# The end of the first norm moved from GpSimd to VectorE, in place, and the first expert's input taken straight from the selection product

## The chip, the cores and the metric

One core of one Trainium2 chip runs the kernel. TensorE multiplies matrices, VectorE and ScalarE work on elements, GpSimd does some element work and issues DMAs, and the sync engine's queue issues the large loads. The metric is device time in microseconds for one execution; lower is better.

## The reference, cut to what matters

One layer on 512 tokens of 1024 features (16 more tokens are prepended and cut off again). Two mixers give `mixed`, and then:

```python
h = layer_norm(ALPHA * h + mixed @ w_out, ln1_g, ln1_b)      # the first norm
logits_g, logits_e = h @ w_rg + b_rg, h @ w_re + b_re        # one of 4 groups, 2 of its 4 experts
...
for e in range(16):
    y = y + gates[:, e:e + 1] * ((silu(h @ w1[e]) * (h @ w3[e])) @ w2[e])
h = layer_norm(ALPHA * h + y, ln2_g, ln2_b)
```

The kernel computes an expert only for the tokens that chose it (up to 128 slots).

## The kernel before, in words

Everything is float32. To multiply at full rate each operand is split into two parts, high and low, and a product is three matmuls (`mm3`, lines 128 to 130). For the experts' weights a split is one ScalarE copy (line 900) and one VectorE subtraction (line 901) of 128 x 1024 elements. The kernel is written in program order under a tile framework, which inserts the waits between engines and whose scheduler orders the instructions of each engine by its own estimates; `issue_after` holds a block of instructions back until a given one.

The stages are: the input projection woven with the first mixer; the second mixer (`stick_breaking`, with scans at line 513 on VectorE) woven with the output projection (`out_proj`); the end of the first norm, the router and the choice of experts; 16 experts; the second norm.

Tokens come in four row blocks of 128. Blocks 3 and 2 end inside the weave, blocks 1 and 0 behind it. For each block `out_second` adds the last half of the projection to the rows `r` (line 743), transposes `r` on TensorE for the router's product (lines 750 to 754), takes mean and deviation (`norm_stats`, lines 249 to 253, with a logarithm and an exponential on ScalarE), corrects the router's logits (lines 757 and 758), and rewrites `r` as (r - mean) / deviation (line 759, VectorE). `out_rows` then makes gain and bias on GpSimd (lines 762 and 763, each 128 x 1024 elements) into another tile, `h1`, and writes it to two arrays in DRAM: `h1d`, from which the experts gather their tokens, and `ad`, to which they add their results. `choose` finds the experts of two blocks (lines 778 to 791, VectorE), `rank` numbers the tokens of an expert (two TensorE matmuls and lines 807 and 809); line 809 builds `sf`, the selection of expert 0's tokens.

Expert 0 does not gather. `first_rows` (line 923, TensorE) multiplies the rows by `sf`, which selects and transposes them at once; line 1197 (VectorE, eight instructions) gives gain and bias to the product, and lines 1199 and 1200 split it into `xh` and `xl`. Expert 1 gathers its tokens by the index of line 957 (line 963, GpSimd), and line 1031 transposes them on TensorE. Behind expert 0's first product all engines pass a branch (line 1088) that handles experts with more than 128 tokens; it reads a count that line 1002 writes, and ScalarE reaches it behind the activation at line 1050.

The weights come in loads of 1 MB on the sync engine's queue (`pump`, line 877) into 15 slots, at most three in flight. A slot is free again when its two parts are split (`split_to`), so the splits set when loads start.

Of the kernel before, what the change touches and what calls it, by code (L numbers as in the profile page):

```python
# [9 lines left out]
F32 = mybir.dt.float32  # L10
# [3 lines left out]
AF = mybir.ActivationFunctionType  # L14
OP = mybir.AluOpType
# [3 lines left out]
P = 128  # L19
D = 1024  # L20
# [3 lines left out]
KC = D // P  # L24
# [21 lines left out]
FIRST = 4  # L46
# [35 lines left out]
def hymba_kernel(ctx: ExitStack, tc: tile.TileContext, x, meta, w_in, lbnd, hgg, sbg, w_out, ln1g, ln1b,  # L82
                 wrg, brg, wre, bre, wg, wu, wd, ln2g, ln2b, out):
    nc = tc.nc
    V = nc.vector
# [4 lines left out]
    def f32(ap):  # L90
        return ap.bitcast(F32)
# [17 lines left out]
    h1d = tc.dram_tile([T, D], F32, name="h1d")  # L109

    ad = tc.dram_tile([T, D], F32, name="ad")
# [79 lines left out]
    for i2 in range(2):  # L191
        xr_ = xr[i2]
        for i1 in range(2):
            i = 2 * i2 + i1
            for hf in range(2):
                p_ = pj([P, 4, P])
# [512 lines left out]
    rt_ = []  # L709
# [29 lines left out]
    def out_second(i, acc, first):  # L739
        r = rt_[i]  # L740
        for hf in range(2):
            cs = slice(hf * 512, hf * 512 + 512)
            V.tensor_add(r[:, cs], r[:, cs], acc[hf])
        if i % 2 == first:
            h1[i], h1[i ^ 1] = (t[:, j] for t in (big_tile(2),) for j in range(2))
        hT = h1[i].rearrange("p (a b) -> p a b", a=KC)
        for hf in range(2):
            p_ = zb([P, 4, P])
            for k in range(4):
                nc.tensor.transpose(p_[:, k, :], r[:, (4 * hf + k) * P:(4 * hf + k + 1) * P], ident)  # L750
            nc.scalar.activation(hT[:, 4 * hf:4 * hf + 4], p_, AF.Copy)
        p_ = zb([P, 20])
        for k in range(KC):
            nc.tensor.matmul(p_, hT[:, k, :], wr[:, k, :], start=(k == 0), stop=(k == KC - 1))
        mu, rstd = norm_stats(r)

        V.scalar_tensor_tensor(lg[:, i, :], nws, mu, p_, op0=OP.mult, op1=OP.add)
        V.scalar_tensor_tensor(lg[:, i, :], lg[:, i, :], rstd, lgb, op0=OP.mult, op1=OP.add)
        V.tensor_scalar(r, r, mu, rstd, op0=OP.subtract, op1=OP.mult)

    def out_rows(i):
        nc.gpsimd.tensor_mul(h1[i], rt_[i], gb1[0])
        nc.gpsimd.tensor_add(h1[i], h1[i], gb1[1])
        nc.gpsimd.dma_start(h1d[i * P:(i + 1) * P, :], h1[i])
        nc.gpsimd.dma_start(ad[i * P:(i + 1) * P, :], h1[i])

    cnt, ohg, M = small("cnt", [NT, 5, 4]), small("ohg", [NT, 4]), small("M", [2, NT, 4, 4])
    Mb = small("Mb", [NT, NE], BF)
# [2 lines left out]
    def choose(i0):  # L771

        sl = slice(i0, i0 + 2)

        l5 = lg[:, sl].rearrange("p i (r j) -> p (i r) j", j=4)
        lj, li = l5[:, :, None, :].to_broadcast([P, 10, 4, 4]), l5[:, :, :, None].to_broadcast([P, 10, 4, 4])
        gt4, ge4 = (ctl.tile([P, 10, 4, 4], F32, tag="gt", bufs=2, name="gt") for _ in range(2))
        V.tensor_tensor(gt4, lj, li, op=OP.is_gt)
        V.tensor_tensor(ge4, lj, li, op=OP.is_ge)
        V.copy_predicated(gt4.rearrange("p a b c -> p a (b c)"),  # L780
                          before.rearrange("p a b -> p (a b)")[:, None, :].to_broadcast([P, 10, 16]),
                          ge4.rearrange("p a b c -> p a (b c)"))
        V.tensor_reduce(cnt[:, sl].rearrange("p i r j -> p (i r) j"), gt4, axis=AX.X, op=OP.add)
        V.tensor_scalar(ohg[:, sl], cnt[:, sl, 0, :], 0.0, None, op0=OP.is_equal)
        ohgb = ohg[:, sl, :, None].to_broadcast([P, 2, 4, 4])
        top = ctl.tile([P, 2, 4, 4], F32, tag="top", bufs=1, name="top")
        V.tensor_scalar(top, cnt[:, sl, 1:5, :], 1.0, None, op0=OP.is_le)
        V.tensor_mul(Mb[:, sl].rearrange("p i (g e) -> p i g e", g=4), top, ohgb)

        V.tensor_scalar(M[:, 1, sl], cnt[:, sl, 1:5, :], 1.0, None, op0=OP.is_equal)  # L790
        V.tensor_mul(M[:, 1, sl], M[:, 1, sl], ohgb)

    r1, sf = small("r1", [NT, NE]), [None, None]

# [20 lines left out]
    def out_proj():  # L815
        gb = big_tile(2)
        gb1.extend((bcast_row(gb[:, 0], ln1g, nc.scalar), bcast_row(gb[:, 1], ln1b, nc.scalar)))
        wo = wo_half(0)
        yield 1
        for i in range(NT):  # L820
            if i % 2 == 0:
                t = big_tile(2)
                rt_.extend((t[:, 0], t[:, 1]))
            nc.sync.dma_start(rt_[i], x[0, i * P:(i + 1) * P, :])
            acc = [zb(), zb()]
            for n_ in range(4):
                wo_mm(i, 0, wo, acc, (n_,))
                if n_ < 3:
                    yield 1
            for hf in range(2):  # L830
                cs = slice(hf * 512, hf * 512 + 512)
                V.scalar_tensor_tensor(rt_[i][:, cs], rt_[i][:, cs], ALPHA, acc[hf], op0=OP.mult, op1=OP.add)
            yield 1
        wo = wo_half(4)
        pump(R_LATE)
        yield 1
        wo2.extend(wo)
        for i in (3, 2):
            acc = [zb(), zb()]
            for n_ in range(4):  # L840
                wo_mm(i, 4, wo, acc, (n_,))
                yield 1
            out_second(i, acc, 1)
            out_rows(i)
            yield 1
        choose(2)
        rank(2)
        pump(R_AFTER)
# [63 lines left out]
    for i in (0, 1):  # L912
        wo_mm(i, 4, wo2, acc2[i], range(EARLY, 4))
    for i in (0, 1):
        out_second(i, acc2[i], 0)

    p1_ = [pj([P, 4, P]) for _ in range(2)]

# [6 lines left out]

    for hf in range(2):
        first_rows(hf, 1)
    choose(0)
    nc.gpsimd.memset(xg, 0.0)
    pump(R_NEXT - at[0])  # L930

# [7 lines left out]
    def select(e):  # L939

        s_ = mp.tile([P, NT, P], BF, tag="sel", bufs=3, name="sel")
        V.tensor_tensor(s_, iow[:, None, :].to_broadcast([P, NT, P]), r1[:, :, e:e + 1].to_broadcast([P, NT, P]),
                        op=OP.is_equal)
        return s_
# [140 lines left out]
    def overflow():  # L1085

        n_max = nc.values_load(cmi[0:1, 0:1], min_val=0, max_val=T)
        with tc.If(n_max > CAP):  # L1088
            with ExitStack() as ov:
# [44 lines left out]
                with tc.For_i(0, NE, 1) as e:  # L1134
                    for c in range(1, T // CAP):
# [40 lines left out]
                                                 scale=osv[:, 1:2].bitcast(F32))  # L1176
                        scatter(y, osv[:, 0:1])

    sel1 = select(1)
    with tc.issue_after(i_.ins):  # L1180
        split_to(FIRST)
    xh = mp.tile([P, KC, P], F32R, tag="xh", bufs=1, name="xh")
    xl = mp.tile([P, KC, P], F32R, tag="xl", bufs=1, name="xl")
    x1 = mp.tile([P, D], F32, tag="y", bufs=1, name="y").rearrange("p (k n) -> p k n", k=KC)
    for hf in range(2):
        first_rows(hf, 0)
        p_ = p1_[hf]
        if hf == 0:
            p1 = slot_sums(1, sel1, slice(0, 2))
            slot_rows(1, p1)  # L1190
            with tc.issue_after(i_.ins):
                out_rows(0)
                out_rows(1)
            gather(xg[:, 1], idx[:, 1:2])
        for k in range(4):
            c = 4 * hf + k
            V.tensor_scalar(x1[:, c], p_[:, k], cp[:, 16 + c:17 + c], cp[:, 24 + c:25 + c], op0=OP.mult, op1=OP.add)
        d_ = slice(4 * hf, 4 * hf + 4)
        nc.scalar.activation(xh[:, d_], x1[:, d_], AF.Copy)
        V.tensor_sub(xl[:, d_], x1[:, d_], f32(xh[:, d_]))  # L1200
    xs[0] = (xh, xl)
    gscr = mp.tile([P, 512], F32, tag="hs", bufs=1, name="gscr")
    gscr = (gscr[:, 0:2 * NT * NE], gscr[:, 2 * NT * NE:4 * NT * NE])
# [216 lines left out]
```

## Time and profile before

| | |
|---|---|
| median of 3 runs | 730.28 us (729.41 to 730.34) |
| the profiled execution | 727.62 us, its span 725.9 us |
| PE (TensorE) busy | 658.3 us, 91% of the span |
| DVE (VectorE) busy | 550.8 us, 76% |
| ACT (ScalarE) busy | 426.0 us, 59% |
| POOL (GpSimd) busy | 189.3 us, 26% |
| DMA | 143.67 MB, mean 198 GB/s |

The profile gives each engine's busy time, the granted TensorE clock, the transfers, and who waited for whom. Busy shares are averages over stages with different limits, so the text reads the stage around the change by itself. A busy VectorE instruction may also be one that is held up: its duration then stands out against the same instruction elsewhere.

### The profile page before, as it was taken

The page shows a single profiled execution, that of the slowest core. Times are in us where ns is not written, and L with a number is a line of the kernel's source. Part 1 is how long each engine was busy: PE and PEld are TensorE (multiplying, and loading weights), DVE is VectorE, ACT ScalarE, POOL GpSimd, SP SyncE. Part 2 cuts the span into 40 slices and gives each one's busy share as a digit, 9 for nine tenths or more (in the row PEclk, how much of TensorE's full clock was granted, in tenths as well). Part 3 has the DMA queues.
Part 4 walks back from the last instruction along what each step waited for, and adds up shares of the span by engine and source line. Part 5 has one row for each costly group of instructions (what it writes and reads, how often), then busy time and mean ns, then how long its engine had stood idle before and what let it go on. Part 6 is the DMA issues. An engine that isn't in the chain of part 4 may idle for free. (4 is left out here: it accounts for less than half of the span.)

```text
span 725.9 us, 9414 instructions
## 1 busy us (share of the span) xinstructions
PE 658.3 (91%) x3366; PEld 530.3 (73%) x3366; DVE 550.8 (76%) x851; ACT 426.0 (59%) x640; POOL 189.3 (26%) x187
## 2 busy tenths in 40 slices
PE   6999999999999999988775799999999999999870
PEld 5878878777877777777665688888778788787650
DVE  5333064655564896999678999999999999999885
ACT  5353243535262674946214588768688686798682
POOL 5101144333243100112352023413114132112213
PEclk9999999999999999999997899999999999999995
DMA  9341111030004870303552899999999999998612
GB/s 348 121 120 58 59 59 58 4 113 1 1 1 163 304 287 0 117 1 119 224 216 99 290 339 339 351 326 368 329 348 377 335 362 334 334 360 280 216 41 114
DMA packets 62307, 143.67 MB, mean 198 GB/s; under 512 B 7370, under 2 KB 7402, under 8 KB 62256
## 3 DMA queue, kind: packets, MB, share of 16 engines
q1 hardware_dynamic: 53600, 128.98, 49.2%
q0 software_dynamic: 5904, 12.82, 6.0%
q10 hardware_dynamic: 2752, 1.22, 0.8%
q8 instruction: 28, 0.46, 0.2%
q14 instruction: 23, 0.19, 0.1%
HBM read 137.01 MB, written 14.68 MB: 209 GB/s over the span
## 5 line engine op out<-in xcount | busy, mean ns | idle before, releaser
L901 DVE TENSOR_TENSOR b<-b 128x1024 fp32r<-128x1024 f32 x192 | 225.2, 1221 | 4.6 <-ACT b L900 4.6
L900 ACT ACTIVATE b<-b 128x1024 fp32r<-128x1024 f32 x192 | 189.5, 1054 | 14.9 <-PE pj L130 12.3
L128 PE MATMUL pj<-b 128*128 128x512 f32 x264 | 108.1, 412 | 3.4 <-ACTq L1088 2.6
L129 PE MATMUL pj<-b 128*128 128x512 f32 x264 | 106.5, 404 | 0.6 <-DVE b L124 0.6
L130 PE MATMUL pj<-b 128*128 128x512 f32 x264 | 106.3, 403 | 0.0
L129 PE MATMUL pj<-b,xl 128*128 128x512 f32 x224 | 87.7, 391 | 2.7 <-DVE xl L1200 2.7
L128 PE MATMUL pj<-b,xh 128*128 128x512 f32 x224 | 89.3, 400 | 0.2 <-ACT b L900 0.2
L130 PE MATMUL pj<-b,xh 128*128 128x512 f32 x224 | 86.3, 401 | 0.5 <-DVE b L901 0.5
L963 POOL DMA_INDIRECT xg<-h1d,idx x15 | 21.9, 1460 | 175.4 <-DVE gate L960 73.0
L128 PEld LDWEIGHTS pj<-b 128*128 128x128 f32 x264 | 50.6, 192 | 14.5 <-ACTq L1088 2.7
L124 DVE TENSOR_TENSOR b<-b 128x1024 fp32r<-128x1024 f32 x24 | 33.1, 1391 | 35.4 <-ACT b L329 31.9
L130 PEld LDWEIGHTS pj<-b 128*128 128x128 f32 x264 | 51.0, 193 | 11.2 <-issue 0.5
L129 PEld LDWEIGHTS pj<-b 128*128 128x128 f32 x264 | 51.1, 194 | 10.9 <-DVE b L124 0.9
L1010 POOL DMA_INDIRECT ad<-y,idx x14 | 46.7, 3334 | 39.8 <-ACT b L900 27.6
L129 PEld LDWEIGHTS pj<-b,xl 128*128 128x128 f32 x224 | 42.1, 188 | 11.6 <-DVE xl L1200 3.1
L130 PEld LDWEIGHTS pj<-b,xh 128*128 128x128 f32 x224 | 42.0, 188 | 11.2 <-DVE b L901 2.6
L329 ACT ACTIVATE b<-b 128x1024 fp32r<-128x1024 f32 x28 | 29.3, 1056 | 35.4 <-PE pj L130 15.2
L128 PEld LDWEIGHTS pj<-b,xh 128*128 128x128 f32 x224 | 42.1, 188 | 9.0 <-ACT b L900 1.5
L626 ACT ACTIVATE zs<-zs 128x512 f32<-128x512 f32 x28 | 17.7, 632 | 48.1 <-POOL zs L625 48.0
L122 POOL TENSOR_TENSOR b<-b 128x1024 fp32r<-128x1024 f32 x8 | 19.6, 2446 | 92.5 <-ACT b L329 73.0
L624 POOL TENSOR_TENSOR zs<-u 128x256 f32<-128x256 f32 x28 | 22.2, 793 | 63.7 <-issue 25.9
L513 DVE TENSOR_TENSOR_SCAN zs<-zs,t 128x528 f32<-128x528 f32 (+3 forms) x32 | 32.8, 1046 | 2.0 <-ACT t L510 1.9
(339 smaller groups left out, 1325.3 us busy)
## 6 DMA issues: line engine op xcount, KB each, us to landing
b<-in_w_exp_gate_dram SPq DMA_DIRECT2D x32, 1024.0 KB, 8.3
b<-in_w_exp_up_dram SPq DMA_DIRECT2D x32, 1024.0 KB, 8.3
b<-in_w_exp_down_dram SPq DMA_DIRECT2D x32, 1024.0 KB, 10.0
b<-in_w_in_dram SPq DMA_DIRECT2D x12, 1024.0 KB, 5.0
b<-in_x_dram SPq DMA_DIRECT2D x8, 512.0 KB, 8.0
b<-in_w_out_dram SPq DMA_DIRECT2D x4, 1024.0 KB
b<-in_w_in_dram SPq DMA_DIRECT2D x4, 512.0 KB
h1d<-b POOLq DMA_DIRECT2D x4, 512.0 KB, 2.9
```

Source lines behind the costliest of these rows:

```text
L122: nc.gpsimd.tensor_sub(dst, src, hi)
L124: V.tensor_sub(dst, src, hi)
L128: nc.tensor.matmul(acc, ah, bh, start=first, stop=False)
L129: nc.tensor.matmul(acc, al, bh, start=False, stop=False)
L130: nc.tensor.matmul(acc, ah, bl, start=False, stop=last)
L329: latest[0] = nc.scalar.activation(wt[:, 0], src, AF.Copy).ins
L513: V.tensor_tensor_scan(cc[:, rv], cc[:, rv], ll[:, rv], 0.0, op0=OP.add, op1=OP.add)
L624: nc.gpsimd.tensor_sub(xv[:, :, 0, :], ref, bv[:, :, 0, :])
L900: nc.scalar.activation(t[:, 0], raw, AF.Copy)
L901: V.tensor_sub(t[:, 1], raw, f32(t[:, 0]))
L963: nc.gpsimd.indirect_dma_start(out=dst, out_offset=None, in_=h1d, in_offset=bass.IndirectOffsetOnAxis(ap=idx, axis=0), bounds_check=T - 1, ...
L1010: nc.gpsimd.indirect_dma_start(out=ad, out_offset=bass.IndirectOffsetOnAxis(ap=idx, axis=0), in_=y, in_offset=None, bounds_check=T - 1, oo ...
```

## The change

Line 759 and the two GpSimd instructions go. In their place VectorE does two instructions on `r` itself: (r - mean) * gain, then * (1 / deviation) + bias; the two DRAM writes read `r`. Blocks 3, 2 and 0 do this right behind their statistics, block 1 behind the instruction of `choose` that marks its experts. The rows that `first_rows` selects are now finished, so line 1197 goes too: `xh` and `xl` are made from the product in PSUM. The first four splits are no longer held back until the rank is known.

```diff
-        V.tensor_scalar(r, r, mu, rstd, op0=OP.subtract, op1=OP.mult)
-
-    def out_rows(i):
-        nc.gpsimd.tensor_mul(h1[i], rt_[i], gb1[0])
-        nc.gpsimd.tensor_add(h1[i], h1[i], gb1[1])
-        nc.gpsimd.dma_start(h1d[i * P:(i + 1) * P, :], h1[i])
-        nc.gpsimd.dma_start(ad[i * P:(i + 1) * P, :], h1[i])
+        return mu, rstd
+
+    def out_rows(i, stats_):
+
+        r, (mu, rstd) = rt_[i], stats_
+        V.scalar_tensor_tensor(r, r, mu, gb1[0], op0=OP.subtract, op1=OP.mult)
+        V.scalar_tensor_tensor(r, r, rstd, gb1[1], op0=OP.mult, op1=OP.add)
+        nc.gpsimd.dma_start(h1d[i * P:(i + 1) * P, :], r)
+        nc.gpsimd.dma_start(ad[i * P:(i + 1) * P, :], r)
...
-            out_second(i, acc, 1)
-            out_rows(i)
+            out_rows(i, out_second(i, acc, 1))
...
-        out_second(i, acc2[i], 0)
+        st_ = out_second(i, acc2[i], 0)
+        if i == 0:
+            out_rows(0, st_)
...
-    choose(0)
+    i_ = choose(0)
+    with tc.issue_after(i_.ins):
+        out_rows(1, st_)
...
+    split_to(FIRST)
     sel1 = select(1)
-    with tc.issue_after(i_.ins):
-        split_to(FIRST)
...
-    x1 = mp.tile([P, D], F32, tag="y", bufs=1, name="y").rearrange("p (k n) -> p k n", k=KC)
     for hf in range(2):
         first_rows(hf, 0)
         p_ = p1_[hf]
+        d_ = slice(4 * hf, 4 * hf + 4)
+        nc.scalar.activation(xh[:, d_], p_, AF.Copy)
+        V.tensor_sub(xl[:, d_], p_, f32(xh[:, d_]))
         if hf == 0:
             p1 = slot_sums(1, sel1, slice(0, 2))
             slot_rows(1, p1)
-            with tc.issue_after(i_.ins):
-                out_rows(0)
-                out_rows(1)
             gather(xg[:, 1], idx[:, 1:2])
-        for k in range(4):
-            c = 4 * hf + k
-            V.tensor_scalar(x1[:, c], p_[:, k], cp[:, 16 + c:17 + c], cp[:, 24 + c:25 + c], op0=OP.mult, op1=OP.add)
-        d_ = slice(4 * hf, 4 * hf + 4)
-        nc.scalar.activation(xh[:, d_], x1[:, d_], AF.Copy)
-        V.tensor_sub(xl[:, d_], x1[:, d_], f32(xh[:, d_]))
```

The scheduler gives each engine a new order around the change. VectorE between the marks of block 1's experts (`Mb`) and the selection of expert 0's tokens (`xg` holds `sf` there), before:

```order
L788 TENSOR_TENSOR Mb<-top,ohg 128x32
L791 TENSOR_TENSOR M<-M,ohg 128x32
L969 TENSOR_TENSOR M<-Mb,M 128x64
L807 SCALAR_TENSOR_TENSOR r_1855<-tr,Mb 128x32
L981 TENSOR_TENSOR gscr<-M,lg 128x64
L809 TENSOR_TENSOR xg<-iow,r_1855 128x256
```

and with the change (lines 790, 810 and 812 were 788, 807 and 809; 764 and 765 are the two new instructions; 975 and 987 belong to the gates):

```order
L790 TENSOR_TENSOR Mb<-top,ohg 128x32
L793 TENSOR_TENSOR M<-M,ohg 128x32
L764 SCALAR_TENSOR_TENSOR b<-b,mv 128x1024
L810 SCALAR_TENSOR_TENSOR r_1855<-tr,Mb 128x32
L765 SCALAR_TENSOR_TENSOR b<-b,mv 128x1024
L812 TENSOR_TENSOR xg<-iow,r_1855 128x256
```

Block 1's two instructions now stand ahead of `sf`.

VectorE where the first half of expert 0's input is made, before (901 is the low half of a weight split, `y` the product with gain and bias, `ci` and `idx` the index of expert 1):

```order
L1197 TENSOR_SCALAR y<-pj,cp 128x128
L957 TENSOR_SCALAR idx<-z,ci 128x1
L1197 TENSOR_SCALAR y<-pj,cp 128x128
L988 RECIPROCAL gw<-gw 128x4
L1197 TENSOR_SCALAR y<-pj,cp 128x128
L901 TENSOR_TENSOR b<-b 128x1024 x2
L1200 TENSOR_TENSOR xl<-y,xh 128x512
```

and with the change (903 was 901, 1194 was 1200, 963 was 957):

```order
L903 TENSOR_TENSOR b<-b 128x1024 x2
L1194 TENSOR_TENSOR xl<-pj,xh 128x512
L961 TENSOR_SCALAR ci<-z,oob 128x1
L903 TENSOR_TENSOR b<-b 128x1024 x2
L962 SCALAR_TENSOR_TENSOR ci<-z,ci 128x1
L1194 TENSOR_TENSOR xl<-pj,xh 128x512
L963 TENSOR_SCALAR idx<-z,ci 128x1
```

The first four weights' splits still stand around the two subtractions, and the index, which stood ahead of all splits, now stands behind four of them.

TensorE where expert 1's tokens are transposed, inside expert 0's 48 matmuls, before:

```order
L129 MATMUL pj<-b,xl 128x512
L130 MATMUL pj<-b,xh 128x512
L1031 MATMUL z<-ident,xg 128x128 x8
L128 MATMUL pj<-b,xh 128x512
L129 MATMUL pj<-b,xl 128x512
```

and with the change (1037 was 1031):

```order
L128 MATMUL pj<-b,xh 128x512
L129 MATMUL pj<-b,xl 128x512
L1037 MATMUL z<-ident,xg 128x128 x8
L130 MATMUL pj<-b,xh 128x512
L128 MATMUL pj<-b,xh 128x512
```

Before, 24 of expert 0's matmuls stand ahead of the transposition; with the change, 32. ScalarE copies 13 splits ahead of the branch in both; VectorE subtracts 11 ahead of it before and 13 with the change, and the selection of expert 2 (line 942, then 948) moves from behind the branch to ahead of it.

## Rows read from the trace of the kernel before

**Rows 1.** Stages: us, busy PE, PEld, DVE, ACT, POOL, granted clock, DMA share, GB/s.

```profile
340.00:350.00 10.00, 8.24 (x58) 6.95 (x57) 9.06 (x16) 5.01 (x12) 4.74 (x2) 1.00 0.48 181
...
380.00:385.00 5.00, 0.00 (x0) 0.00 (x0) 4.94 (x9) 0.22 (x1) 4.62 (x3) 0.59 0.40 162
...
400.00:420.00 20.00, 16.13 (x75) 12.42 (x74) 18.97 (x40) 10.88 (x12) 2.97 (x2) 0.83 0.82 294
...
440.00:460.00 20.00, 20.00 (x98) 16.45 (x97) 19.38 (x24) 16.95 (x20) 8.38 (x3) 1.00 1.00 343
```

**Rows 2.** Whom TensorE waited for, 372 to 412 us: total, times, longest.

```profile
PE tr L800 <- DVE Mb L788: 9.4, 1, 9.4
```

**Rows 3.** Timeline, VectorE and GpSimd, 374 to 386 us, and two unhindered instructions.

```profile
344.04 0.24 DVE L758 SCALAR_TENSOR_TENSOR lg<-lg,mv,lgb 128x20 f32<-128x20 f32 x1
...
354.07 0.33 DVE L780 COPY_PREDICATED gt<-before,gt 128x160 f32<-128x160 int32 x1
...
374.32 0.23 DVE L757 SCALAR_TENSOR_TENSOR lg<-nws,mv,z 128x20 f32<-128x20 f32 x1 [1.13 <-PE z L754]
...
375.64 2.40 DVE L758 SCALAR_TENSOR_TENSOR lg<-lg,mv,lgb 128x20 f32<-128x20 f32 x1
375.66 2.34 POOL L763 TENSOR_TENSOR b<-b 128x1024 f32<-128x1024 f32 x1
...
379.27 2.73 DVE L780 COPY_PREDICATED gt<-before,gt 128x160 f32<-128x160 int32 x1
...
381.88 2.34 POOL L763 TENSOR_TENSOR b<-b 128x1024 f32<-128x1024 f32 x1
381.91 2.33 DVE L974 TENSOR_TENSOR ge<-lg,gm 128x16 f32<-128x16 f32 x1
...
385.76 0.43 DVE L809 TENSOR_TENSOR xg<-iow,r 128x256 f32<-128x256 f32 x1
```

**Rows 4.** Timeline, VectorE's pairs of scans in the weave; the third runs alone.

```profile
323.65 3.23 DVE L513 TENSOR_TENSOR_SCAN zs<-zs,t 128x144 f32<-128x144 f32 x2
...
328.05 1.91 DVE L513 TENSOR_TENSOR_SCAN zs<-zs,t 128x144 f32<-128x144 f32 x2
...
330.98 1.06 DVE L513 TENSOR_TENSOR_SCAN zs<-zs,t 128x144 f32<-128x144 f32 x2
...
344.93 3.21 DVE L513 TENSOR_TENSOR_SCAN zs<-zs,t 128x144 f32<-128x144 f32 x2
...
348.87 2.36 DVE L513 TENSOR_TENSOR_SCAN zs<-zs,t 128x144 f32<-128x144 f32 x2
```

**Rows 5.** VectorE's groups by form: count | busy us, mean ns | idle before.

```profile
L1345 DVE SCALAR_TENSOR_TENSOR b<-b,st 128x1024 f32<-128x1024 f32 x6 | 7.7, 1277 | 0.1
...
L759 DVE TENSOR_SCALAR b<-b,mv 128x1024 f32<-128x1024 f32 x4 | 3.2, 804 | 0.0
...
L1197 DVE TENSOR_SCALAR y<-pj,cp 128x128 f32<-128x128 f32 x8 | 3.1, 406 | 2.6 <-PE pj L923 2.6
```

**Rows 6.** The page's costliest groups: the low half of a split.

```profile
L901 DVE TENSOR_TENSOR b<-b 128x1024 fp32r<-128x1024 f32 x192 | 225.2, 1221 | 4.6 <-ACT b L900 4.6
```

**Rows 7.** Timeline, TensorE from the selection to the branch; idle before, and its releaser.

```profile
386.24 3.78 PE L923 MATMUL pj<-xg,b 128*128 128x128 f32 x16 [0.72 <-DVE xg L809]
...
389.97 2.58 PE L923 MATMUL pj<-xg,b 128*128 128x128 f32 x16
...
395.92 0.50 PE L129 MATMUL pj<-b,xl 128*128 128x512 f32 x1 [2.66 <-DVE xl L1200]
...
401.08 1.03 PE L1031 MATMUL z<-ident,xg 128*128 128x128 f32 x8
...
410.77 0.50 PE L128 MATMUL pj<-b 128*128 128x512 f32 x1 [2.63 <-ACTq L1088]
```

**Rows 8.** The loads' queue: two loads, the second held up for a slot.

```profile
366.98 30.73 SPq L877 DMA_DIRECT2D b<-in_w_exp_down_dram  x2
```

**Rows 9.** The experts' gathers (tile xg): from issue to landing.

```profile
DMA to landing us min/median/max: 4.2/7.7/8.6
```

More of the change, by code (lines that the diff above doesn't have):

```diff
@@ L787, in choose @@
         V.tensor_scalar(top, cnt[:, sl, 1:5, :], 1.0, None, op0=OP.is_le)
-        V.tensor_mul(Mb[:, sl].rearrange("p i (g e) -> p i g e", g=4), top, ohgb)
+        i_ = V.tensor_mul(Mb[:, sl].rearrange("p i (g e) -> p i g e", g=4), top, ohgb)
         V.tensor_scalar(M[:, 1, sl], cnt[:, sl, 1:5, :], 1.0, None, op0=OP.is_equal)
         V.tensor_mul(M[:, 1, sl], M[:, 1, sl], ohgb)
+        return i_
     r1, sf = small("r1", [NT, NE]), [None, None]
```

## The prediction

> **What bounds the kernel now.** I read the stages first (busy time by stretch), then who waited for whom at the hand-over to the experts, then the timeline there, and last the queue of the loads.
>
> In the experts' stage everything is nearly full: of 20 us TensorE is busy 20.00, VectorE 19.38, and the transfers' share is 1.00 [rows 1]. Nothing this change touches repeats there, so that stage can only move as a block. Ahead of it is a gap. From 380 to 385 us TensorE does nothing [rows 1]; the waits name one releaser, the marks of the experts, with 9.4 us in one piece [rows 2]. The timeline says why they are late. VectorE's line 758 works on 20 elements and takes 2.40 us, where it took 0.24 at 344 us; it starts and ends with GpSimd's line 763. Line 780 takes 2.73 us instead of 0.33 and ends as the next GpSimd instruction begins; line 974, 2.33 us for 16 elements, starts and ends with that one [rows 3]. So VectorE is not working there; it is held by GpSimd's eight 128 x 1024 instructions. In the weave the pairs of scans show the same: 1.06 us alone, and 3.23, 1.91, 3.21 and 2.36 us around the `out_rows` of blocks 3 and 2 [rows 4]. VectorE is busy 9.06 of 10 us there [rows 1], so holds count there too.
>
> The loads stop as well: the queue's second of two loads from 366.98 leaves 30.73 us later, at 397.7 [rows 8], when the third split has freed a slot.
>
> **The change, step by step.** The sum is made against the profiled execution, 727.6 us with 725.9 of span; the median of the runs is 730.3, 2.7 above it, and I add that at the end.
>
> *A. Blocks 3 and 2, in the weave.* The holds that go: 3.23 + 1.91 + 3.21 + 2.36 less four times 1.06, 6.5 us [rows 4]. Line 759 goes twice, 2 x 0.80 = 1.6. Four new instructions come. The nearest row is line 1345, the same operation and size at 1.28 us [rows 5], line 901 has 1.22 [rows 6]; I take 1.25, so 5.0. Together -3.1 us on a VectorE that bounds this stretch. If the scheduler's new order there eats it, 0; a loss is rival three's. I take -3.1, since VectorE is the full engine there; from 0 to -3.1.
>
> *B. Blocks 0 and 1, to the selection of expert 0.* Block 0's two instructions (2.5 us for 0.8) stand ahead of block 1's statistics: 1.7 us later, of which VectorE's idle 1.13 in front of line 757 [rows 3] can absorb part; the logarithm and exponential on ScalarE stand in between, so I let 0.7 be absorbed: +1.0 (0.6 to 1.7). Then the holds go: 2.40 - 0.24, 2.73 - 0.33, and 2.33 less 0.24 for an instruction of that size, together -6.6 [rows 3]. Block 1's line 759 goes, -0.8 [rows 5]. Its two new ones stand ahead of `sf`, +2.5; the two `rank` matmuls lie beside the first of them. Sum -3.9: the selection is built at 381.8 instead of 385.76 [rows 3].
>
> *C. From the selection to expert 0's matmuls.* The eight line 1197 go, 8 x 0.41 = 3.2 us [rows 5], and of those the ones ahead of the first `xl` were on the path. What is late next is TensorE itself: `first_rows` took 3.78 us at a half-speed clock, then 2.58 us [rows 7]; the granted clock was 0.59 over 380 to 385 [rows 1]. Kept as they are, and with the two matmuls that need no `xl`, the stream of matmuls begins at 381.8 + 0.5 + 3.8 + 2.6 + 0.7 = 389.4. VectorE is not later: from the selection it has six small instructions and two splits of 1.22 [rows 6], some 5 us by estimate, so the first `xl` is ready near 387.5, behind ScalarE's copy of the product. Before, the stream began at 395.92, with a wait for `xl` [rows 7]. So B and C give -6.5, C alone -2.6. At full clock C would be 2 us better.
>
> *D. Up to the branch.* ScalarE's way there is 13 split copies behind or around the transposed tokens of expert 1. These now stand behind 32 matmuls, not 24. From 395.92 to 401.08 there are 22, 0.235 us each [rows 7], so 8 x 0.235 = +1.9: transposition at 396.4. The index for their gather stands behind four splits now, near 391.2; issued at 391.3, it must land within 5.1 us. The least landing is 4.2, the median 7.7 [rows 9]; the median belongs to gathers among a full stream of loads, here two loads have just been issued. I take 5.5, nearer the least: +0.4 (0 to 3.5; rival two). The DRAM writes of the rows move with the rows and start some 6 us earlier than now, and GpSimd's queue, without its eight instructions, only waits; the gather finds them done. The splits that reuse the rows' tiles wait for the same writes and come later still.
>
> *E. Behind the branch.* TensorE restarts after 2.63 us of idleness [rows 7]; a further wait for expert 2's selection goes, because that now stands ahead of the branch, as do two more splits. I take -1.0 us for that, an estimate inside the 2.63 that TensorE idled. Between 400 and 420 the clock was 0.83 [rows 1], 3.4 us lost; if it stays up, -4.4, if the additional work on VectorE's queue is in the way, 0.
>
> *F. The experts and the end.* Unchanged work, moved as a block: 0. The cover is that the loads restart early too: the third split ends near 389.1 less A, 386.0, for 397.7 [rows 8], 11.7 us sooner, more than TensorE gains, so the stream of weights is no new wait.
>
> Sum: -3.1 - 3.9 - 2.6 + 2.3 - 1.0 = -8.3 us. 727.6 becomes 719.3 in a profile, the median **722.0**.
>
> F is where a rule speaks another way. The rows have transfers at a share of 1.00 and 343 GB/s [rows 1], and TensorE without a gap in the same stretch; I follow TensorE, the smaller gain. The Trainium skill, "SBUF — State Buffer", section "A bandwidth-pool intuition that's wrong (but worth ruling out)", says HBM is almost always the end-to-end bottleneck, at about 358 GB/s; by it the end would move with the first loads alone, which is rival one, 718.6 against my 722.0.
>
> **The rivals.** A measurement of this kernel tells 0.2%, 1.5 us, from no change.
>
> *One: the stream of weights alone sets the end.* For it: the share of 1.00. Against it: TensorE, also full. Then all of the earlier restart counts: 730.3 - 11.7 = 718.6. Chance 0.17.
>
> *Two: the gather is late.* For it: the median of 7.7 us, the longest 8.6 [rows 9], and that the loads restart just ahead of it. Against it: only two of them can. At 8.6 the tokens of expert 1 land at 399.9, 3.5 us behind their place; ScalarE's copies and the branch wait, and the sum is 3.1 us worse than mine, 725.1. It decides from 5.1 us of landing on. Chance 0.16.
>
> *Three, the other side: GpSimd is not what holds VectorE.* If those instructions are long for another reason (late operands that the trace books as busy), the holds stay and only work is added: A +3.4 (5.0 - 1.6), B +2.7 (1.0 - 0.8 + 2.5), C -2.6, D +2.3: +5.8, 736.1. For it: no row names GpSimd as a releaser. Against it: three instructions of quite different work, two of which start and end with GpSimd's within 0.1 us, and the same lines short elsewhere [rows 3]. It decides from about half the holds on. Chance 0.05.
>
> *Four: the gap is refilled.* The change doesn't do what it says if expert 0 then waits for something else just as long, its weights' splits above all, for ScalarE's copies of them may stand behind what `xh` waits for. Then C, D and E undo B, and only part of A is left, within 1 us of 730. Against it: the first four splits have nothing left to wait for but their loads, landed 15 us before. Chance 0.04.
>
> **How the numbers follow.** My forecast has 0.58, the likeliest case. Its own unknowns run from A = 0 and E = 0 (726.1) to E = -4.4, a full clock in C and no wait in D (716.2). The range that holds 8 of 10 takes in most of these, rivals one and two, and some of two together with a lost A (728.2): 716.5 to 727.5. Faster by over 0.2% is the forecast with rivals one and two, 0.91; no change is rival four with a little of two, 0.04; slower is rival three, 0.05.
>
> **What would show it.** In the new profile: lines 758, 782 (was 780) and 980 (was 974) at 0.2 to 0.4 us, and the pairs of scans at 1.06: A and B right. The new lines 764 and 765 near 1.25 us. TensorE's wait for the marks nearer 3 us than 9.4, and its stream for expert 0 beginning 9 to 10 us sooner, near 386: B and C. Line 1037 right behind its matmul, without a wait for the gather: D; with one, rival two. The branch passed 7 to 8 us sooner and no wait for a selection behind it: E. The experts' stage at the same pace per expert, 340 to 350 GB/s: F. Line 758 still at 2 us with no GpSimd instruction beside it makes the prediction wrong at its root; an unchanged branch with an early stream makes D wrong; a longer experts' stage makes F wrong.

## The result, and the profile after

| | before | after |
|---|---|---|
| median of 4 runs, in one comparison | 729.85 us (727.88 to 730.34) | 720.51 us (718.70 to 722.11) |
| ratio | | 0.987, 95% interval 0.9841 to 0.9899 |
| profiled execution, its span | 727.62, 725.9 us | 718.70, 717.0 us |
| DVE busy, POOL busy | 550.8, 189.3 us | 540.7, 164.4 us |

The forecast was 722.0 us. The profile came down by 8.9 us where the steps summed to 8.3, but the terms did not come out one by one: the first gave twice what it was counted for, the next two somewhat more, and the stretch behind them took part of it back.

Stages of the kernel after, with the columns of [rows 1]; the empty stretch of TensorE lies at 370 to 375 now:

```profile
340.00:350.00 10.00, 9.21 (x54) 7.48 (x54) 9.46 (x24) 5.97 (x14) 0.97 (x2) 1.00 0.27 104
370.00:375.00 5.00, 0.77 (x10) 0.68 (x10) 5.00 (x18) 2.11 (x3) 0.50 (x1) 0.60 0.28 113
...
390.00:400.00 10.00, 7.63 (x24) 6.05 (x24) 5.86 (x11) 5.99 (x8) 0.00 (x0) 0.66 0.38 116
400.00:420.00 20.00, 14.80 (x79) 12.26 (x80) 17.17 (x32) 11.74 (x15) 2.02 (x2) 0.91 0.71 244
440.00:460.00 20.00, 20.00 (x102) 16.29 (x101) 18.80 (x28) 16.95 (x20) 7.69 (x2) 1.00 1.01 350
```

The experts' stage is as full as before. New is 390 to 400: TensorE with gaps and a clock of 0.66. Whom TensorE waited for, 362 to 408 us (total, times, longest); the 9.4 us of [rows 2] are the third line here:

```profile
PE z L1037 <- DMA xg<-h1d,idx: 4.8, 1, 4.8
PE z L955 <- DVEq L1094: 4.2, 1, 4.2
PE tr L803 <- DVE Mb L790: 2.6, 1, 2.6
PE pj L927 <- DVE xg L812: 2.6, 1, 2.6
```

VectorE's timeline answers to [rows 3, 4]: from 318 us to the experts no instruction takes noticeably longer than the same one elsewhere, and the new lines 764 and 765 take 1.28 us each.

```profile
323.66 1.07 DVE L513 TENSOR_TENSOR_SCAN zs<-zs,t 128x144 f32<-128x144 f32 x2
...
344.99 1.06 DVE L513 TENSOR_TENSOR_SCAN zs<-zs,t 128x144 f32<-128x144 f32 x2
...
363.85 0.23 DVE L757 SCALAR_TENSOR_TENSOR lg<-nws,mv,z 128x20 f32<-128x20 f32 x1 [1.58 <-PE z L754]
...
366.06 0.22 DVE L758 SCALAR_TENSOR_TENSOR lg<-lg,mv,lgb 128x20 f32<-128x20 f32 x1
366.19 1.28 DVE L765 SCALAR_TENSOR_TENSOR b<-b,mv 128x1024 f32<-128x1024 f32 x1
...
370.32 0.34 DVE L782 COPY_PREDICATED gt<-before,gt 128x160 f32<-128x160 int32 x1
370.56 0.17 DVE L980 TENSOR_TENSOR ge<-lg,gm 128x16 f32<-128x16 f32 x1
...
374.12 0.42 DVE L812 TENSOR_TENSOR xg<-iow,r 128x256 f32<-128x256 f32 x1
```

TensorE's timeline answers to [rows 7]: the selection product, the stream for expert 0, the transposition of expert 1's tokens behind a wait, the restart behind the branch.

```profile
374.59 3.59 PE L927 MATMUL pj<-xg,b 128*128 128x128 f32 x16 [2.59 <-DVE xg L812]
...
378.12 2.03 PE L927 MATMUL pj<-xg,b 128*128 128x128 f32 x16
...
380.45 0.39 PE L129 MATMUL pj<-b,xl 128*128 128x512 f32 x1
...
392.21 1.97 PE L1037 MATMUL z<-ident,xg 128*128 128x128 f32 x8 [4.79 <-DMA xg<-h1d,idx]
...
405.55 0.38 PE L955 MATMUL z<-vals,sel 128*128 128x5 bf16 x8 [4.16 <-DVEq L1094]
```

The sync engine's queue and GpSimd's, the restarted loads and the gather of expert 1's tokens:

```profile
381.10 0.37 SPq L879 DMA_DIRECT2D b<-in_w_exp_down_dram  x1
382.24 0.37 SPq L879 DMA_DIRECT2D b<-in_w_exp_gate_dram  x1
...
383.84 1.54 POOL L969 DMA_INDIRECT xg<-h1d,idx  x1 [8.29 <-DVE dm L1221]
```

and that gather in the list of transfers, with the time from issue to landing at the end:

```profile
xg<-h1d,idx POOLq DMA_INDIRECT x1, 8.3
```

It was issued at 383.84 and landed 8.3 us later, against 4.2 before (the least of [rows 9]).

So the selection comes 11.6 us sooner than before (374.12 for 385.76), but the first activation's transposition, line 1074, only 8.1 sooner (412.62 for 420.74). My theory: GpSimd's reads had held VectorE, which gave the 11.6; 3.5 us then went to the late gather and to the branch. Rivals: GpSimd isn't the cause, or the stream of weights sets the end.

### The profile page after: what moved, and what is told of

Read it like the earlier page. It is cut to its first block, busy times and chain, and to the rows that moved or that the text cites. A ratio compares the mean times of both kernels' runs of the same rounds, so it can differ in the third digit from the quotient of the medians.

```text
span 717.0 us, 9402 instructions
## 1 busy us (share of the span) xinstructions
PE 656.4 (92%) x3366; PEld 530.0 (74%) x3366; DVE 540.7 (75%) x847; ACT 425.5 (59%) x640; POOL 164.4 (23%) x179
## 5 line engine op out<-in xcount | busy, mean ns | idle before, releaser
L128 PE MATMUL pj<-b,xh 128*128 128x512 f32 x224 | 90.5, 405 | 0.2 <-ACT b L902 0.2
L130 PE MATMUL pj<-b,xh 128*128 128x512 f32 x224 | 87.5, 407 | 0.5 <-DVE b L903 0.5
L128 PEld LDWEIGHTS pj<-b 128*128 128x128 f32 x264 | 50.3, 191 | 11.7 <-DVE b L201 0.8
L130 PEld LDWEIGHTS pj<-b 128*128 128x128 f32 x264 | 50.3, 191 | 11.0 <-issue 0.5
L129 PEld LDWEIGHTS pj<-b 128*128 128x128 f32 x264 | 50.3, 191 | 10.6 <-DVE b L124 0.9
L1016 POOL DMA_INDIRECT ad<-y,idx x14 | 42.5, 3037 | 39.1 <-ACT b L902 28.3
L130 PEld LDWEIGHTS pj<-b,xh 128*128 128x128 f32 x224 | 42.7, 191 | 11.4 <-DVE b L903 2.6
L128 PEld LDWEIGHTS pj<-b,xh 128*128 128x128 f32 x224 | 42.9, 192 | 9.0 <-ACT b L902 1.5
L122 POOL TENSOR_TENSOR b<-b 128x1024 fp32r<-128x1024 f32 x8 | 19.6, 2448 | 91.1 <-ACT b L329 71.5
L627 DVE TENSOR_TENSOR zs<-zs,u 128x256 f32<-128x256 f32 x28 | 13.3, 474 | 25.0 <-ACT zs L626 25.0
## 6 DMA issues: line engine op xcount, KB each, us to landing
b<-in_w_exp_down_dram SPq DMA_DIRECT2D x32, 1024.0 KB, 10.2
```

What stands on the lines that cost most here:

```text
L122: nc.gpsimd.tensor_sub(dst, src, hi)
L128: nc.tensor.matmul(acc, ah, bh, start=first, stop=False)
L129: nc.tensor.matmul(acc, al, bh, start=False, stop=False)
L130: nc.tensor.matmul(acc, ah, bl, start=False, stop=last)
L1016: nc.gpsimd.indirect_dma_start(out=ad, out_offset=bass.IndirectOffsetOnAxis(ap=idx, axis=0), in_=y, in_offset=None, bounds_check=T - 1, oo ...
```

## The experiments

Each was timed beside the kernel before on one chip; its ratio and 95% interval stand with the median.

**1 and 2. GpSimd's instructions put back as dead work, and writes of the same length.** Block 1 is left out, since its instructions would stand ahead of the gather on GpSimd's queue.

```diff
+        d_ = nc.gpsimd.dma_start(ad[i * P:(i + 1) * P, :], r)
+        if i != 1:
+            with tc.issue_after(d_.ins):
+                nc.gpsimd.tensor_mul(h1[i], r, gb1[0])
+                nc.gpsimd.tensor_add(h1[i], h1[i], gb1[1])
```

(The first line was there; new is its name, `d_`.)

> The kernel after, with GpSimd's two 128 x 1024 instructions put back for blocks 3, 2 and 0, behind the two DRAM writes; what they make goes to the dead tile h1 and is read by nobody, so nothing waits for them. My theory (GpSimd instructions that read SBUF hold VectorE): the pairs of scans beside them take 1.9 to 3.2 us again instead of 1.06, small VectorE instructions of block 1's statistics or choice take some 2.3 us instead of 0.2, the selection of expert 0 comes 6 to 11 us later (6.5 from the weave, up to 4.4 behind block 0), and the time is 726 to 731 us. Rival three of the prediction (GpSimd isn't what holds VectorE): nothing waits for the new instructions, so all lines stay short and the time stays within 1.5 us of 720.5.

In the second run the last two lines are five `nc.gpsimd.memset(h1[i], 0.0)`.

> The kernel after, with five GpSimd memsets of 128 x 1024 elements (some 4.7 us together) in the places where the run beside it has GpSimd's two instructions that read: GpSimd just as busy, but it only writes SBUF. If any long GpSimd instruction holds VectorE, this run is as slow as the one with reads, 726 to 731 us. The Trainium skill, page SBUF - State Buffer, section Who interferes with whom, has VectorE instructions with two SBUF inputs contend with GpSimd only where GpSimd reads SBUF: by it the scans stay at 1.06 us and the time within 1.5 us of 720.5. I take the second.

Measured: 733.62 us with the reads (1.0062, 1.002 to 1.0103), 719.6 with the writes (0.9882, 0.9846 to 0.9918). Timeline with the reads, VectorE and GpSimd:

```profile
329.18 5.12 DVE L513 TENSOR_TENSOR_SCAN zs<-zs,t 128x144 f32<-128x144 f32 x2
...
379.78 2.35 POOL L770 TENSOR_TENSOR b<-b 128x1024 f32<-128x1024 f32 x1
...
380.13 2.02 DVE L243 SCALAR_TENSOR_TENSOR mv<-mv 128x1 f32<-128x1 f32 x1
382.19 2.39 DVE L758 SCALAR_TENSOR_TENSOR lg<-lg,mv,lgb 128x20 f32<-128x20 f32 x1
382.21 2.34 POOL L771 TENSOR_TENSOR b<-b 128x1024 f32<-128x1024 f32 x1
```

and with the writes:

```profile
368.69 4.00 POOL L771 MEMSET b<- 128x1024 f32 x4
...
369.13 0.16 DVE L243 SCALAR_TENSOR_TENSOR mv<-mv 128x1 f32<-128x1 f32 x1
369.33 0.24 DVE L758 SCALAR_TENSOR_TENSOR lg<-lg,mv,lgb 128x20 f32<-128x20 f32 x1
```

Nobody waits for the added work, and yet line 243, on one element a partition, ends with GpSimd's instruction, as line 758 does. Beside writes both are short. This shows the holds, and that reading is what holds. The Trainium skill, "SBUF — State Buffer", section "Who interferes with whom", states just that: a VectorE instruction with two SBUF inputs contends with a GpSimd instruction that reads SBUF, not with one that only writes. The traces agree. The size was off: 733.62 us for an expected 726 to 731, and the selection came 14.9 us later than after (389.02 for 374.12) for an expected 6 to 11. Block 0's line 757 comes at 374.74 there, 10.9 us later than after, though the one pair of held scans accounts for 4.06. Much of the rest is read below under A.

**3. That part alone, in the kernel before.** Still into `h1`, still behind the rank for blocks 0 and 1:

```diff
-        nc.gpsimd.tensor_mul(h1[i], rt_[i], gb1[0])
-        nc.gpsimd.tensor_add(h1[i], h1[i], gb1[1])
+        V.tensor_mul(h1[i], rt_[i], gb1[0])
+        V.tensor_add(h1[i], h1[i], gb1[1])
```

> The kernel before, with one part of the change alone: the gain and the bias of the first norm on VectorE (two 128 x 1024 instructions a block, at some 1.22 us) instead of GpSimd, into the same tile and still behind the rank for blocks 0 and 1; line 759, the eight line 1197 and the order stay. My theory: the holds go (6.5 us in the weave, 6.6 us at the marks of the experts), four instructions come into the weave (4.9) and four behind the selection (4.9, of which some lies beside the selection product): 729.9 - 1.6 - 6.6 + 0 to 4.9, so 722 to 727 us, nearest 724. Rival three (no hold by GpSimd): only work is added, 731 to 735 us. If nearly all of the change's gain came from the terms C to E instead, this run stays at 728 to 730.

Measured: 724.61 us (0.9946, 0.9924 to 0.9969), as expected; rival three is out. The selection comes at 376.26, 9.5 us sooner than before, and from it to the first activation's transposition it takes 41.6 us instead of 35.0, with the four instructions in that stretch.

**4. The gather ahead of the splits and of the selection product.**

```diff
+    sel1 = select(1)
+    p1 = slot_sums(1, sel1, slice(0, 2))
+    slot_rows(1, p1)
+    gather(xg[:, 1], idx[:, 1:2])
     split_to(FIRST)
-    sel1 = select(1)
...
-        if hf == 0:
-            p1 = slot_sums(1, sel1, slice(0, 2))
-            slot_rows(1, p1)
-            gather(xg[:, 1], idx[:, 1:2])
```

> The kernel after, with the index and the gather of expert 1's tokens written ahead of the first four splits and of the selection product of expert 0, instead of behind the product's first half. The theory (rival two's mechanism is at work in the kernel after: the gather is issued beside the restarted loads and lands 8.3 us later): issued near 378.5, with no loads running, it lands in 4.2 to 5 us, by 383.5, ahead of the transposition near 386; TensorE's wait of 4.8 us goes and with it the half clock behind it, the branch is passed 5 to 8 us sooner, and the time is 713 to 716 us. Rival: the gather takes 8 us by itself, whatever runs beside it; then it lands near 386.5 and gives 717 to 718. Second rival: what counts is the stream of weights, whose restart this does not move; then 719.5 to 721.5.

Measured: 715.95 us (0.9818, 0.9785 to 0.9852). Timeline, the gather's issue and TensorE:

```profile
380.42 1.24 POOL L969 DMA_INDIRECT xg<-h1d,idx  x1 [2.96 <-DVE idx L963]
...
387.98 1.03 PE L1037 MATMUL z<-ident,xg 128*128 128x128 f32 x8
...
401.50 0.38 PE L955 MATMUL z<-vals,sel 128*128 128x5 bf16 x8 [4.16 <-DVEq L1094]
```

```profile
xg<-h1d,idx POOLq DMA_INDIRECT x1, 4.5
```

Issued 3.1 us ahead of the first load (383.50), it lands in 4.5; line 1037 waits for nothing and runs at full clock. From selection to restart 25.5 us instead of 31.4. The late gather is shown to be the loss of term D. The 4.16 us at the branch stay.

**5. Term C undone in the kernel after.**

```diff
+        for k in range(4):
+            V.tensor_scalar(x1[:, 4 * hf + k], p_[:, k], 1.0, 0.0, op0=OP.mult, op1=OP.add)
-        nc.scalar.activation(xh[:, d_], p_, AF.Copy)
-        V.tensor_sub(xl[:, d_], p_, f32(xh[:, d_]))
+        nc.scalar.activation(xh[:, d_], x1[:, d_], AF.Copy)
+        V.tensor_sub(xl[:, d_], x1[:, d_], f32(xh[:, d_]))
```

> The kernel after, with eight VectorE instructions of the size of line 1197 put back between the selection product and its two parts (they multiply by 1 and add 0, so values stay). This undoes the main part of term C. My theory: TensorE's stream for expert 0 begins 2 to 3.5 us later (the eight took 406 ns each), but expert 1's tokens land near 392 all the same, so the loss is hidden in TensorE's 4.8 us of waiting for them: 720 to 722 us. Rival: the start of the stream counts for the end, then it costs what C gave, 3 to 4 us: 723.5 to 724.5.

Measured: 718.14 us (0.9832, 0.9793 to 0.9871): not slower than the kernel after, if anything faster, though the intervals overlap. TensorE:

```profile
384.23 0.50 PE L129 MATMUL pj<-b,xl 128*128 128x512 f32 x1 [0.22 <-DVE xl L1197]
...
391.16 1.09 PE L1037 MATMUL z<-ident,xg 128*128 128x128 f32 x8 [1.38 <-DMA xg<-h1d,idx]
...
401.60 0.36 PE L955 MATMUL z<-vals,sel 128*128 128x5 bf16 x8 [3.67 <-DVEq L1094]
```

The stream starts 9.0 us behind the selection (375.21) instead of 6.3, as expected, and yet TensorE is past the branch after 26.4 us instead of 31.4. Waiting less, it kept its clock (1.09 us for the transposition, 1.97 after), and the scheduler put only four split copies, not six, between expert 1's tokens and the activation. So in the kernel after the eight instructions' removal gives nothing at the end. That was expected; that the run is, if anything, faster was not: 718.14 lies below the expected 720 to 722.

**6. A load held until the gather has landed.** A wait of the next load behind the first `pump` of the splits:

```diff
+                if n_ == R_NEXT:
+                    tc.add_manual_dep(loads[n_], g1[0].name, ...)
```

> The kernel after, where the first load that restarts the stream of weights waits until expert 1's tokens have landed. The stream restarts some 7 us later, near 388.5 instead of 381.1, and the gather has the transfers to itself. Contention theory: the gather lands in 4.2 to 4.6 us instead of 8.3, TensorE's wait shrinks from 4.8 to 1 to 2.5 us. Forecast's term F (TensorE sets the end, the stream has room to spare): the end gains what TensorE gains, 716 to 718.5 us. Rival one (the stream of weights alone sets the end): the end moves with the first load, 726 to 729 us. If the gather is slow by itself, it lands after 8 us here too, the stream restarts near 392 and the time is 721 to 731.

Measured: 718.63 us (0.9852, 0.9824 to 0.988). It held less than meant: the two loads that restart the stream were in the queue already and went at 381.55 and 382.68; the third went at 390.87 instead of 386.96. The gather, issued 4.3 us behind the first load, landed in 4.9. TensorE's wait was 2.04 us. That the time did not rise with a later third load speaks against rival one; the strong form of the test was not made.

**7. Splits 12 and 13 and the next fetches behind the activation's product** (`held` is that product on VectorE, and the activation on ScalarE; for expert 1's first part, `fetch(2)` and `fetch(3)`):

```diff
+            with tc.issue_after(held[0].ins), tc.issue_after(held[1].ins):
+                up(e, (0,), acc)
```

> The kernel after, with the 12th and 13th split and the fetch of experts 2 and 3 held behind the product of expert 0's activation, so that VectorE does 11 splits ahead of the branch, as in the kernel before. This tests term E: in the kernel after VectorE is the last at the branch, at 405.45 us, and ScalarE's activation has ended by 402.91. My theory: the work put ahead of the branch is what TensorE waits for there; VectorE passes near 403.2 and the time falls by 2 to 2.5 us, to 717.5 to 719 us. Rival: TensorE then waits behind the branch for the same splits, and the time stays at 720 to 721.

Measured: 718.24 us (0.9846, 0.9829 to 0.9864), inside what was expected. It is 0.24% under the kernel after by the ratios, but the intervals overlap, so the time alone doesn't show a gain. TensorE's restart:

```profile
403.30 0.79 PE L128 MATMUL pj<-b 128*128 128x512 f32 x1 [2.60 <-ACTq L1095]
```

From expert 1's transposition (392.29) to there it takes 11.0 us instead of 13.3. Part of it is paid back behind the branch: to the first line 1074 it is 19.0 us instead of 20.4. The run isn't clean, for its transposition took 1.09 us and not 1.97, and here too only four split copies, not six, stand between expert 1's tokens and the activation.

**8, 9 and 10. Together, and with a fourth edit.**

> Both: the gather of expert 1 ahead of the first splits, and the 12th and 13th split behind the branch. If TensorE's way sets the end, the branch is passed some 3 us sooner than with the early gather alone, and the time is 712 to 714 us. If with the early gather the stream of weights has become the bound (rival one, from there on), nothing more is gained: 715 to 717 us.

Measured: 715.1 us (0.9815, 0.9782 to 0.9847). The stretch from the selection to line 1074's counterpart is 31.8 us against 32.8 in run 4: 1.0 us gained, not 3. ScalarE shows why:

```profile
396.42 1.28 ACT L1056 ACT_TABLE_LOAD   x1 [3.60 <-DVE vals L1002]
```

The activation is written to the tile that the gates used as scratch, and waits for VectorE's gate values. Run 10 moves those ahead (`with tc.issue_after(v_.ins): transposed(1, ...)`, `v_` the last of the gate values). Run 9 and run 10 also try the end. There the chain of the kernel after reads:

```profile
652.91 9.77 DMA ad<-y,idx
662.76 0.70 ACT y L1085
```

Expert 13's result waits for the scatter of expert 12's, which is in the same tile. The step that this lengthens is the one from expert 13's line 1074 to expert 14's (652.20 to 671.05 in the kernel after); the expectations below call it the step to the last expert, one too late.

```diff
-        y = mp.tile([P, D], F32, tag="y", bufs=1, name="y")
+        y = big_tile(2)[:, 0] if e == NE - 2 else mp.tile([P, D], F32, tag="y", bufs=1, name="y")
```

> The kernel after, with one thing changed that the change under study does not touch: the result of the last expert but one gets a tile of its own, so that ScalarE's line 1085 no longer waits until the scatter of the expert before it has landed. In eight profiles so far the step from the last expert but one to the last (TensorE's first transposition of the activations, line 1074) took 9.08 us plus the time in which that scatter landed (8.3 to 10.8 us), 18.85 us in the kernel after. Theory (the scatter's landing, not the stream of weights, sets the end): the step falls to 17 to 17.5 us, the matmuls' own time, the time to 718.5 to 719.3 us, and the runs spread less than 718.7 to 722.1. Rival (the weights of the last expert come no sooner): the step stays at 18 us or more and the time within 0.7 us of 720.5.

> The early gather, the splits behind the branch, the tile of its own for the last result but one, and the gate values finished on VectorE ahead of the low half of expert 1's tokens (their scratch is the tile that the activation of expert 0 is written to; in the run with the first two alone ScalarE waited 3.6 us for it). Theory: TensorE's way sets the end throughout; against that run the branch is passed some 2 us sooner and the last step is 1 to 1.5 us shorter: 711 to 713 us. Rival (the stream of weights has become the bound): no better than it, 714.5 to 716.

Measured: 720.95 us (0.9886, 0.9866 to 0.9905) and 715.56 us (0.9831, 0.9808 to 0.9855). Run 9 gave the tile to the wrong result: expert 14's has no wait there. The step stayed at 18.20 us, 9.08 plus a landing of 9.12. Run 10 has the shortest stretch behind the selection, 31.5 us, and no better time than run 8; 715.56 lies above the expected 711 to 713.

**11 and 12. The same for expert 13's result,** in the kernel after and in run 10's, which returned expert 14's to its old tile:

```diff
+        if e == NE - 3:
+            y = mp.tile([P, KC, P], F32R, tag="xh", bufs=1, name="y")...
```

> The run before changed the wrong result: ScalarE's line 1085 and VectorE's line 1086 that wait for a scatter write the result of expert 13 (of 0 to 15), over the result of expert 12, whose scatter was issued at 653.57 us and landed 9.12 later. Here the result of expert 13 gets a tile of its own, in the kernel after. Theory (that landing sets the step to the last expert, 9.08 us plus the landing in nine profiles): both instructions run when TensorE has the product, some 2 us sooner, the step falls from 18 to 19 to 16.5 to 17.5 us, and the time to 718 to 719.3 us. Rival (the step is set by something else that ends at the same time): the step stays over 18 us and the time at 720.5 within 0.8 us.

> The early gather, the splits behind the branch, the gate values ahead of the low half of expert 1's tokens, and the tile of its own for the result of expert 13. Theory: the scatter's landing took back up to 2 us of what the first three gave; without it 712.5 to 714.3 us. Rival (the stream of weights is the bound by now): 715 to 716.

Measured: 729.56 us (0.9996, 0.9974 to 1.0018) and 724.72 us (0.9942, 0.9928 to 0.9956), 9 us worse than without. Timeline of run 11, TensorE and VectorE:

```profile
653.69 0.66 PE L1074 MATMUL tr<-ident,hs 128*128 128x128 f32 x4 [1.25 <-DVE y L1089]
...
670.40 0.66 PE L1074 MATMUL tr<-ident,hs 128*128 128x128 f32 x4
...
685.44 1.28 DVE L1385 TENSOR_TENSOR b<-b,z 128x512 f32<-128x512 f32 x2 [6.65 <-DMA b<-ad,idx]
...
687.91 0.80 PE L130 MATMUL pj<-b 128*128 128x512 f32 x1 [6.90 <-DVE b L903]
```

The step did what was said, 16.7 us instead of 18 to 19. But the scheduler now put line 1385, which waits for the sums gathered from DRAM, ahead of the last ten splits on VectorE, and TensorE waited 6.9 us for the first of them. The landing sets that step, then; what its removal is worth with the old order was not tried.

Runs 4, 8 and 10 are below both kernels (0.9815 to 0.9831 against 0.987), but each interval overlaps that of the kernel after a little, by 0.0011, 0.0006 and 0.0014. All executions of runs 4 and 8 (at most 718.14 us) are under the fastest of the kernel after (718.70), though in other comparisons. Run 8 is the lowest; the three aren't told apart.

## Why the prediction came out right, step by step

| Step | place | forecast | profile |
|---|---|---|---|
| A | block 0's line 757, 370.52 to 363.85 | -3.1 (0 to -3.1) | -6.7 |
| B | from there to the selection | -3.9 | -5.0 |
| C | selection to TensorE's stream, 10.2 to 6.3 us | -2.6 | -3.8 |
| D | stream to expert 1's transposition, 5.2 to 11.8 | +2.3 (+1.9 to +5.4) | +6.6 |
| E | transposition to the first line 1074, 19.7 to 20.4 | -1.0 (0 to -4.4) | +0.8 |
| F | the experts and the end | 0 | -0.8 |
| sum | | -8.3 | -8.9 |

The time is right, and the cause of A and B is shown by runs 1 to 3. But that the sum is this close is luck: 6.7 us of gain that was not foreseen (A, B, C, F) met 6.1 us of loss that was not (D, E).

**A failed in size,** outside its own bounds. Stages from 318 us to block 0's line 757, before:

```profile
318.00:370.52 52.52, 45.64 (x290) 38.23 (x289) 41.75 (x95) 21.84 (x53) 14.44 (x9) 0.97 0.47 170
```

and after:

```profile
318.00:363.85 45.85, 43.74 (x289) 37.20 (x289) 38.14 (x96) 22.31 (x52) 4.21 (x5) 1.00 0.50 176
```

VectorE's busy time fell from 41.75 to 38.14, by 3.6: about the term as it was counted. The other 3.1 us was VectorE's idle time, 10.8 to 7.7. It lies behind block 2's rows: up to block 2's line 757 (341.29 before, 339.75 after) the gain was 1.5 us for 1.3 counted, from there to block 0's 5.1 for 1.8. "-3.1, since VectorE is the full engine there" left out what a hold does to the other engine. Stages of the kernel before, behind block 2's rows:

```profile
344.00:352.00 8.00, 4.72 (x28) 3.59 (x26) 7.96 (x13) 2.67 (x7) 6.15 (x4) 1.00 0.40 146
352.00:360.00 8.00, 6.96 (x34) 6.03 (x34) 4.00 (x17) 1.33 (x4) 0.00 (x0) 0.79 0.65 249
```

the same of the kernel after:

```profile
344.00:352.00 8.00, 7.21 (x42) 5.91 (x40) 7.83 (x26) 2.38 (x6) 1.06 (x2) 1.00 0.29 63
352.00:360.00 8.00, 7.63 (x46) 6.09 (x45) 3.79 (x10) 1.27 (x4) 1.81 (x1) 1.00 0.95 355
```

and of run 1, where reads were put back:

```profile
328.00:336.00 8.00, 4.13 (x18) 3.03 (x17) 8.00 (x11) 2.60 (x5) 5.63 (x4) 0.92 0.66 246
336.00:344.00 8.00, 6.99 (x30) 6.49 (x31) 5.04 (x13) 1.76 (x4) 0.00 (x0) 0.50 0.04 16
```

While VectorE is held TensorE idles (4.72 of 8 us busy, 4.13 in run 1), and behind that it was granted 0.79 and 0.50 of its clock (0.50 is the lower level, 1.2 GHz). Beside the writes of run 2 it was busy 7.08 of 8 us over 328 to 336 and had 1.00 there and behind. VectorE then waits for the slow TensorE: for line 544 it waited 2.9 us in one piece before, 0.9 at the most after. How the 3.1 us divide between the lower clock and the order of the work was not tested. The clock of 0.83 over 350 to 360 stood in the trace of before and was not read.

**B** was right in mechanism and 1.1 us small; lines 758 and 980 are at 0.17 to 0.24 us and 782 at 0.34, as forecast. Of the 1.1, 0.4 is a hold that was not counted: line 243 took 0.57 us before and 0.16 after. **C** gave 1.2 us more: the second half of TensorE's product, kept at 2.58 us, took 2.03, and the first `xl` was not waited for. By run 5 that gain is worth nothing at the end, since the stream then waits for the gather.

**D failed at its landing.** The eight more matmuls took 1.8 us, as counted. The issue came where it was put (9.5 us behind the selection in the working, 9.7 in the trace), but "here two loads have just been issued. I take 5.5" measured 8.3. Rival two's mechanism happened, and larger than it priced, as C made the stream end sooner: TensorE waited 4.8 us, and from 390 to 400 its clock was 0.66. Run 4 shows it: without the wait the stretch from selection to restart is 5.9 us shorter.

**E failed in sign.** Behind the branch the gain came, and more than was taken: from the restart to the first line 1074 7.1 us for 10.0, without the wait for expert 2's selection and back at full clock after 3 us for 7.5. But up to the restart it took 13.3 us for 9.7. The two more splits ahead of the branch were seen, and their cost was given as the bound 0; they made VectorE the last engine there. ScalarE's activation and VectorE's 13th split:

```profile
402.31 0.60 ACT L1056 ACTIVATE hs<-pj 128x512 f32<-128x512 f32 x1
...
404.23 1.22 DVE L903 TENSOR_TENSOR b<-b 128x1024 fp32r<-128x1024 f32 x1
```

The split ends at 405.45, 2.5 us behind the activation (402.91); before, the activation came last (410.67), 0.8 us behind the last split. Run 7, with 11 splits ahead, had 11.0 us from transposition to restart for 13.3. The other 1.1 us is ScalarE's: its activation ended 10.7 us behind the transposition for 9.6, with six split copies in between in both kernels; about half of that is the transposition at half clock (1.97 us for 1.03).

**F and rival one.** The pace per expert is unchanged: line 1074 came three times at 17.98 us, before at 17.94. The -0.8 lies in two steps near the end: the one from expert 13's line 1074 to expert 14's took 0.7 us more and the next one 1.6 us less. Both vary by 2.5 us and more between the runs (last section), so it says nothing of the change. The loads restarted 16.2 us sooner (381.10 for 397.34; 11.7 were forecast) and the end moved 8.9; so the first loads alone don't set it. The Trainium skill's rule that HBM is almost always the bottleneck ("SBUF — State Buffer", section "A bandwidth-pool intuition that's wrong (but worth ruling out)") would have had the end follow them; here it did not. Why run 10, 1.3 us faster than run 4 from the selection to the first line 1074, is no faster in its median stays open; the two steps read in the last section vary by more than that.

## What to carry to other kernels

A short VectorE instruction that takes as long as a GpSimd instruction beside it is held, not slow; moving the GpSimd work costs VectorE its price and gives back the holds, and TensorE's clock behind them too. Where a stretch is shortened, look for the DMA whose cover was the length of the stretch: a gather that had room before must be issued earlier by as much. And count what the new order puts ahead of a point that all engines pass: the engine that comes last sets it, and being early on another is worth nothing there.

## What the hardware showed that I had not expected

The landing of the same gather of 128 rows, by when it was issued. Alone, or some 3 us ahead of the loads: 4.2 us (before), 4.5 (runs 4 and 8), 4.7 (run 10), 4.4 (run 12). Between 2.2 and 2.9 us behind the first of two 1 MB loads: 8.3 (after), 8.1 (run 11), 7.6 (run 3), 7.4 (run 2), 7.2 (run 1), 7.0 (run 7), 6.9 (runs 5 and 9). At 4.3 us behind it: 4.9 (run 6). So it lands late beside loads that have just begun, and two are enough: in run 3 the third load starts only when the gather has landed. By what means wasn't tested.

The step from expert 13's line 1074 to expert 14's was 9.08 us plus the landing of expert 12's scatter, within 0.01 us, in all twelve profiles in which the two results share a tile: 17.37 us with 8.30 (run 2), 18.11 with 9.03 (before), 18.85 with 9.77 (after), 19.89 with 10.81 (run 4). One DMA's landing, which varied by 2.5 us between executions, thus passes straight into that step. The next step, to the last expert, goes by TensorE's clock: in the same profiles it took 17.3 us where 1.00 was granted (after, runs 2 and 3), 18.4 to 18.9 at 0.91 (before, runs 1, 5, 7, 8 and 9) and 19.6 to 19.9 at 0.83 to 0.84 (runs 4, 6 and 10). Together they make effects of 1 us hard to see in medians.
